# Weight-sum transfers queued behind the attention, and a first chunk that takes the high halves first

## The chip, the cores and the metric

The kernel runs on one core of one Trainium2 chip. The metric is the device time of one execution in microseconds (us), the median of three runs. The engines are named as in the profile: PE (TensorE, matrix products), PEld (its weight loads), DVE (VectorE), ACT (ScalarE), POOL (GpSimd), and SP (SyncE), which here only issues transfers.

## The reference

One residual decoder block on 512 tokens of width 1024, all in float32: a SwiGLU layer, a mixer, and a second SwiGLU layer, each between two RMS norms.

```python
f = swiglu(rms_norm(h, ffn1_pre_g), ffn1_w_gu, ffn1_w_down)     # D_FF = 2816
h = h + 0.5 * rms_norm(f, ffn1_post_g)
m = hybrid_mixer(rms_norm(h, mix_pre_g), ...)
h = h + rms_norm(m, mix_post_g)
f = swiglu(rms_norm(h, ffn2_pre_g), ffn2_w_gu, ffn2_w_down)
h = h + 0.5 * rms_norm(f, ffn2_post_g)

def hybrid_mixer(u, ...):
    gate, x, q, k, v, g_lru, g_attn = split(u @ w_in)            # 1024 1024 1024 256 256 1024 1024
    y_lru = rg_lru(causal_depthwise_conv(x)) * gelu(gate)
    y_attn = sliding_window_attention_with_sinks(rope(q), rope(k), v)   # window 128, 16 heads, 4 key heads
    merged = sigmoid(g_lru) * (y_lru @ w_proj_lru) + sigmoid(g_attn) * (y_attn @ w_proj_attn)
    return merged @ w_out
```

## The kernel before, in words

**Numbers in two halves.** Every operand of a product is split into a high half (rounded to the matrix engine's float32 form) and a low half (the rest). A product of a weight `w` and activations `u` is three matmuls into one PSUM bank: high by high (line 167), high weight by low activation (168), low weight by high activation (169). This is `mm3`.

**Weights.** They are streamed from HBM in pieces of 128 x 1024 in one fixed order, `worder`. `wload` issues the transfer of a piece into `wraw` from SP's queue (line 105), `wround` casts it to the high half on ACT (line 115), `wsplit` subtracts for the low half on DVE (line 123). `wget` and `wnow` hand out the next pair and keep a few pieces ahead. The number in `w85` or `wraw85` is the place in that order.

**Stages.** First feed-forward layer; a token-wise boundary (norms, then transposition of the normalised tokens into features, `to_features`: eight transposes on PE at line 227, a cast on ACT at 231 for `u2h`, a subtraction on DVE at 232 for `u2l`); the mixer's products with `u2`; the output projection `woX`; a second boundary that makes `u3h` and `u3l`; the second feed-forward layer. The boundaries `b1` and `b2` go through four blocks of 128 tokens, so the features of early tokens are ready while later ones are still in work. For this the first chunks of the next layer (a chunk is 128 output columns, eight pieces of the contraction) are done over the tokens' halves of 256: `first_four` for the mixer's `x` products, `first_six` for the second feed-forward layer's `f2f`. Both call `feat_chunk`, which goes through the eight pieces with the three matmuls of `mm3` at each.

**The mixer's order.** `x`, `k`, `v`, `q0` and `q1`, then eight `gate` chunks, then `q2` and `q3`, then eight `gl` chunks (gate and projection of the recurrent branch: `glg`, `glp`), then eight `ga` chunks (of the attention: `gag`, `gap`), then the output projection. `q_pair` sends its rotated result to DRAM and back in another layout, from SP's queue: a store `q_halves` (line 966) and, when that has landed, four loads into `qt` (line 971). A generator `attend(g, n)` does one attention block, of head group `g` and token block `n`: scores on PE (`at30b` is group 3, block 0; line 988), exponentials on ACT, the normalisation of the scores on POOL (line 1003, `at30s`), transposes and the product with `v`, whose upper half ACT copies (`at03c`) and DVE adds to `ya`; `split_y` then splits `ya` for the `ga` stage. The blocks of groups 0 and 1 are started in the `gate` stage and with `q2`, those of groups 2 and 3 in the `gl` stage; the last is `at33`.

**Sums of weights.** The output projection and the feed-forward layers' second products are done by a scheme with seven products in place of eight, which needs sums of weight blocks. For the output projection there are four, `osum[0]` to `osum[3]`, in DRAM, 1 MB each. They are made by transfers alone:

```python
oplan = ((0, 2, 0), (2, 3, 2), (1, 3, None), (3, 1, None))
```

For `(o, a, b)`, block `a` of `w_o` is copied to `osum[o]`, and then block `b` of it, or `osum[o // 2]` where `b` is None, is added by an accumulating transfer. So `osum[1]` needs `osum[0]` complete, and `osum[3]` needs `osum[1]`. The copies are issued from SP's queue in the `gl` chunks 2 to 5 (line 1107, behind the weight load that was issued last), the accumulations from POOL's queue in the `ga` chunks 0, 2 and 4 (line 1147). They are read again as weights: `osum[1]` first, for the second of the output projection's products.

**What sets the order.** Each engine goes through its own queue in order. The program's scheduler sets the order of the queues from the program text, its dependencies and estimates of its own. `tc.issue_after(i)` keeps what stands under it behind instruction `i`. In the parts that the change touches, POOL has little besides the score normalisations and, at the boundaries, some powers (`rstd`, line 212).

Of the kernel before, what the change touches and what calls it, by code (L numbers as in the profile page):

```python
# [11 lines left out]
ALU = mybir.AluOpType  # L12
# [4 lines left out]
P = 128  # L17
# [24 lines left out]
def hybrid_block_kernel(ctx, tc, x, xt, g1, w_first, gains, gu1, gs1, dn1, w_x, w_gate, w_q, w_k, w_v, w_gl, w_ga, w_pl, w_pa,  # L42
# [191 lines left out]
                keep.append((raw[half][:, :, ts_], bv))  # L234
        return [lambda z=z, bv=bv: A.copy(z, bv) for z, bv in keep]

    def feat_chunk(b, w, u, tok):
        wh, wl = w
        for k in range(KD):
            ks = slice(k * P, (k + 1) * P)  # L240
            mm3(b[:, tok], wh[:, ks], wl[:, ks], at(u, 0, k, tok), at(u, 1, k, tok), k == 0, k == KD - 1)
# [4 lines left out]
    def first_four(u, name, done):  # L246
        first = []
        for i in range(4):
            first.append((wget(), bank(f"{name}{i}")))
        for tok in HALVES:  # L250
            for i, (w, b) in enumerate(first):
                feat_chunk(b, w, u, tok)
                tick()
                if tok is HALVES[1]:
                    done(i, b)

    def first_six(u, name, done, early):
        first = []
        for i in range(6):
            first.append((wnow(), bank(f"{name}{i}")))  # L260
            if i < 5:
                wsplit(wpos[0] + 1)
            feat_chunk(first[i][1], first[i][0], u, HALVES[0])
            tick()
        for i, (w, b) in enumerate(first):
            if i == 2:
                early()
            if i >= 4:
                wsplit(wpos[0] + i - 3)
            feat_chunk(b, w, u, HALVES[1])  # L270
            tick()
            done(i, b)

# [621 lines left out]
    def x_group(gi):  # L895
        a4, m4, bx4 = (b8(f"{n}{gi}", [P, 4, T]) for n in ("la", "lm", "lb"))
        hl.append(m4)
        cr = range(4 * gi, 4 * gi + 4)
        if gi == 0:
            first_four(u2, "x", lambda c, b: start(lru_chunk(c, b, a4, m4, bx4, c == cr[-1])))  # L900
        else:
            for c in cr:
                w = wget()
                b = bank(f"x{c}")
                feat_chunk(b, w, u2, ALL)
                tick()
                start(lru_chunk(c, b, a4, m4, bx4, c == cr[-1]))
# [66 lines left out]
    def attend(g, n, kp, vt, y):  # L974
        nm = f"at{g}{n}"
        nk = 1 if n == 0 else 2
        W = nk * P
        keys = slice((n - nk + 1) * P, (n + 1) * P)
        s = t4(f"{nm}s")[:, :4 * W].rearrange("p (h w) -> p h w", h=4)
        sk = sink[:, 4 * g:4 * g + 4]  # L980
        mx = sm(f"{nm}m", 4)
        for half in range(2):
            b = bank(f"{nm}b{half}")
            for i in range(2):
                q = qts[g][:, 2 * half + i, n * P:(n + 1) * P]
                o = b[:, i * W:(i + 1) * W]
                for sgn in range(2):
                    PE.matmul(o, lhsT=q, rhs=kp[g // 2][:, g % 2, sgn, keys], start=sgn == 0, stop=sgn == 1)
            for i in range(2):
                j = 2 * half + i  # L990
                V.tensor_tensor_reduce(out=s[:, j, :], in0=b[:, i * W:(i + 1) * W], in1=msk[:, 2 * P - W:],
                                       scale=HD ** -0.5, scalar=sk[:, j:j + 1], op0=ALU.add, op1=ALU.max,
                                       accum_out=mx[:, j:j + 1])
        es = sm(f"{nm}e", 4)
        V.tensor_tensor(out=es, in0=sk, in1=mx, op=ALU.subtract)
        V.tensor_scalar_mul(mx, mx, -1.0)
        ss = sm(f"{nm}ss", 4)
        for j in range(4):
            A.activation(s[:, j, :], s[:, j, :], AF.Exp, bias=mx[:, j:j + 1], accum_out=ss[:, j:j + 1])
        A.activation(es, es, AF.Exp)  # L1000
        V.tensor_tensor(out=ss, in0=ss, in1=es, op=ALU.add)
        V.reciprocal(ss, ss)
        G.tensor_tensor(out=s, in0=s, in1=ss.rearrange("p (h o) -> p h o", o=1).broadcast_to([P, 4, W]), op=ALU.mult)
        yield ATT_LAG[0]
        pt = []
        for kb in range(nk):
            b = bank(f"{nm}t{kb}")
            for j in range(4):
                PE.transpose(out=b[:, j * P:(j + 1) * P], in_=s[:, j, kb * P:(kb + 1) * P], identity=ident)
            ph, pl = t2(f"{nm}ph{kb}", F32R), t2(f"{nm}pl{kb}", F32R)  # L1010
            A.copy(ph, b)
            V.tensor_tensor(out=pl, in0=b, in1=ph.bitcast(F32), op=ALU.subtract)
            pt.append((ph, pl))
        yield ATT_LAG[1]
        o = bank(f"{nm}o")
        for kb in range(nk):
            v = vt[:, n - nk + 1 + kb, g].rearrange("p s e -> p (s e)")
            for i in range(2):
                PE.matmul(o, lhsT=v, rhs=pt[kb][i], start=kb + i == 0, stop=kb + i == nk)
        r = g % 2  # L1020
        own, oth = slice(HD * r, HD * r + HD), slice(HD * (1 - r), HD * (1 - r) + HD)
        tmp = t2(f"{nm}c")
        A.copy(tmp[own, :], o[oth, :])
        V.tensor_tensor(out=y[own, :, n * P:(n + 1) * P], in0=o[own, :].rearrange("p (h q) -> p h q", h=4),
                        in1=tmp[own, :].rearrange("p (h q) -> p h q", h=4), op=ALU.add)
# [34 lines left out]
        return s, b  # L1060

    qts = {}
    x_group(0)
    kp = [b8(f"kp{i}", [P, 2, 2, T], F32R) for i in range(2)]
    vt = b8("vt", [P, NT, NKV, 2, HD], F32R)
# [32 lines left out]
    for c in range(KD):  # L1098
        s, b = sig_gate(c, yl, "gl")
        if c % 4 == 0:  # L1100
            m1.append(b8(f"m1{c}", [P, 4, T]))
        V.scalar_tensor_tensor(out=m1[-1][:, c % 4, :], in0=s, scalar=1.0, in1=b, op0=ALU.add, op1=ALU.mult)
        if c == 2:
            start(split_y(y0, "ya0"))
        if 2 <= c < 6:
            with tc.issue_after(wdma[wpos[0]].ins):
                SP.dma_start(osum[oplan[c - 2][0]], w_o[oplan[c - 2][1]])
        next_attend()
        if c % 2 == 1:
            next_attend()  # L1110
# [30 lines left out]
    for c in range(KD):  # L1141
        s, b = sig_gate(c, ya, "ga")
        V.scalar_tensor_tensor(out=s, in0=s, scalar=1.0, in1=b, op0=ALU.add, op1=ALU.mult)  # L1143
        V.tensor_tensor(out=mg[c // 4][:, c % 4, :], in0=s, in1=m1[c // 4][:, c % 4, :], op=ALU.add)
        if c % 2 == 0 and c < 6:
            for o, _, b in (oplan[:2], oplan[2:3], oplan[3:])[c // 2]:
                G.dma_start(osum[o], osum[o // 2] if b is None else w_o[b], accum_op=ALU.add)
        if c == 4:
            oop_split(1, a11)
        if c == 5:  # L1150
            oop_split(7, osum_tile("os3", a11, a21, ALU.subtract))
            oop_split(2, a12, ks=slice(0, 2))
# [213 lines left out]
```

## Time and profile before

| | |
|---|---|
| median of three runs | 1121.56 us (1121.44, 1121.56, 1122.51) |
| the profiled execution | 1122.35 us |
| its span in the trace | 1120.6 us, 16935 instructions |
| mean granted clock of PE | 0.996 |
| busy share of the span | PE 98%, PEld 88%, DVE 80%, ACT 54%, POOL 7% |
| moved between HBM and the core | 238 GB/s over the span |

The time of the profiled execution is 1.75 us longer than the span, which goes from its first instruction to its last. The granted clock is the share of full speed that PE was given. In rows on single instructions the first two numbers are the start and the duration in us, then come engine, line, operation, output and inputs, and in brackets the wait ahead of it with what ended it. In a row of the timeline one group may stand for several instructions (x8). In rows of transfers the last numbers are KB and us from issue to landing. `SPq` and `POOLq` are the queues of transfers that SP and POOL issue.

### The profile page before, as it was taken

What the parts mean: (1) busy time and instruction counts of PE and PEld (TensorE: products, weight loads), DVE (VectorE), ACT (ScalarE), POOL (GpSimd) and SP (SyncE); (2) the same over time, 40 slices, a digit from 0 to 9 for tenths busy, and PEclk for the clock granted to TensorE, in tenths of its full rate; (3) what the DMA queues carried; (4) which work ended last, traced back from release to release, by engine and by line L of the source; (5) the groups of instructions that cost most, each with busy time, mean ns of one, the idle gap of its engine ahead of it and who ended that gap; (6) DMA issues with size and microseconds to landing.
All of it is one profiled execution on the core that took longest, in us unless ns stands there. A gap on an engine that the chain in (4) does not pass through costs nothing. (4 is left out here: it accounts for less than half of the span.)

```text
span 1120.6 us, 16935 instructions
## 1 busy us (share of the span) xinstructions
PE 1102.9 (98%) x6582; PEld 982.5 (88%) x6582; DVE 899.9 (80%) x1357; ACT 602.3 (54%) x1003; POOL 83.0 (7%) x86
## 2 busy tenths in 40 slices
PE   9999999999999999999899999999999999999997
PEld 7889999988878888788688888888999999998885
DVE  6998898889998788988656561579789889888896
ACT  7445555465664757675545441257444455456562
POOL 1000010000000101122122000001000000000000
PEclk9999999999999999999989999999999999999999
DMA  9239999664677173612983440446339999555483
GB/s 362 81 121 263 303 288 301 186 225 132 224 274 263 39 207 115 167 57 101 304 230 108 151 156 22 122 146 240 132 99 284 314 272 307 136 161 189 149 275 118
DMA packets 55295, 213.60 MB, mean 191 GB/s; under 512 B 6576, under 2 KB 6704, under 8 KB 49456
## 3 DMA queue, kind: packets, MB, share of 16 engines
q1 hardware_dynamic: 46864, 171.11, 45.0%
q0 software_dynamic: 4032, 27.26, 12.3%
q10 hardware_dynamic: 4320, 14.16, 3.5%
q8 instruction: 51, 0.84, 0.3%
q14 instruction: 28, 0.23, 0.1%
HBM read 200.98 MB, written 66.06 MB: 238 GB/s over the span
## 5 line engine op out<-in xcount | busy, mean ns | idle before, releaser
L123 DVE TENSOR_TENSOR w<-wraw,w 128x1024 fp32r<-128x1024 f32 x174 | 204.2, 1194 | 24.7 <-ACT w L115 24.4
L115 ACT CAST w<-wraw 128x1024 fp32r<-128x1024 f32 x174 | 169.0, 1012 | 29.4 <-PE glp L169 7.4
L169 PE MATMUL f1X<-u1m,f1W 128*128 128x256 f32 x256 | 72.5, 283 | 0.1
L168 PE MATMUL f1X<-u1m,f1W 128*128 128x256 f32 x256 | 72.4, 283 | 0.0
L167 PE MATMUL f1X<-u1m,f1W 128*128 128x256 f32 x256 | 72.4, 283 | 0.0
L169 PEld LDWEIGHTS f1X<-u1m,f1W 128*128 128x128 f32 x256 | 49.1, 192 | 0.3 <-DVE f1W L361 0.3
L167 PEld LDWEIGHTS f1X<-u1m,f1W 128*128 128x128 f32 x256 | 49.1, 192 | 0.1
L168 PEld LDWEIGHTS f1X<-u1m,f1W 128*128 128x128 f32 x256 | 49.1, 192 | 0.1
L1143 DVE SCALAR_TENSOR_TENSOR gas<-gas,gap 128x512 f32<-128x512 f32 x8 | 5.5, 688 | 45.2 <-PE gap L169 45.2
L169 PE MATMUL f2X<-u3m,f2W 128*128 128x256 f32 x144 | 40.9, 284 | 0.1
L169 PE MATMUL f2X<-u3h,f2W 128*128 128x256 f32 x144 | 40.8, 283 | 0.0
L167 PE MATMUL f2Q<-u3m,f2W 128*128 128x256 f32 x144 | 40.8, 283 | 0.0
L168 PE MATMUL f2Q<-u3m,f2W 128*128 128x256 f32 x144 | 40.8, 283 | 0.0
L169 PE MATMUL f2Q<-u3m,f2W 128*128 128x256 f32 x144 | 40.8, 283 | 0.0
L168 PE MATMUL f2X<-u3l,f2W 128*128 128x256 f32 x144 | 40.8, 283 | 0.0
L167 PE MATMUL f2X<-u3m,f2W 128*128 128x256 f32 x144 | 40.8, 283 | 0.0
L168 PE MATMUL f2X<-u3m,f2W 128*128 128x256 f32 x144 | 40.7, 283 | 0.0
L167 PE MATMUL f2X<-u3h,f2W 128*128 128x256 f32 x144 | 40.7, 283 | 0.0
L167 PE MATMUL f1Q<-u1m,f1W 128*128 128x256 f32 x128 | 36.2, 283 | 0.0
L168 PE MATMUL f1Q<-u1m,f1W 128*128 128x256 f32 x128 | 36.2, 283 | 0.0
L169 PE MATMUL f1Q<-u1m,f1W 128*128 128x256 f32 x128 | 36.2, 283 | 0.0
L168 PE MATMUL f1X<-w,f1y 128*128 128x512 f32 x88 | 34.5, 392 | 0.4 <-DVE w L123 0.4
(867 smaller groups left out, 3802.4 us busy)
## 6 DMA issues: line engine op xcount, KB each, us to landing
wraw<-wsum SPq DMA_DIRECT2D x40, 512.0 KB, 4.3
wsum<-in_dn_dram SPq DMA_DIRECT2D x16, 1024.0 KB, 10.5
wraw<-in_dn_dram SPq DMA_DIRECT2D x30, 512.0 KB, 4.8
f2L<-in_gs_dram SPq DMA_DIRECT2D x18, 512.0 KB, 5.3
f2R<-in_gs_dram SPq DMA_DIRECT2D x18, 512.0 KB, 5.2
wraw<-in_gu_dram SPq DMA_DIRECT2D x16, 512.0 KB, 7.3
f1L<-in_gs_dram SPq DMA_DIRECT2D x16, 512.0 KB, 5.8
f1R<-in_gs_dram SPq DMA_DIRECT2D x16, 512.0 KB, 5.8
```

The costliest lines, as they stand in the source:

```text
L115: A.copy(w[:, 0, :], raws[n])
L123: V.tensor_tensor(out=w[:, 1, :], in0=raws[n], in1=w[:, 0, :].bitcast(F32), op=ALU.subtract)
L167: PE.matmul(o, lhsT=ah, rhs=bh, start=start, stop=False, skip_group_check=reopen)
L168: PE.matmul(o, lhsT=ah, rhs=bl, start=False, stop=False, skip_group_check=reopen)
L169: PE.matmul(o, lhsT=al, rhs=bh, start=False, stop=stop, skip_group_check=reopen)
L1143: V.scalar_tensor_tensor(out=s, in0=s, scalar=1.0, in1=b, op0=ALU.add, op1=ALU.mult)
```

## The change

It has two parts.

**The copies.** SP no longer issues the four copies of `w_o` blocks. POOL does, in the `ga` chunks 0 to 3, under `issue_after` of `norms[-1]`, which is the last score normalisation, `at33s`. The accumulations stay on POOL, one each in the `ga` chunks 1, 2, 3 and 5.

**The first chunk.** `feat_chunk` has a new form, `low_last`: over the eight pieces of the contraction it does high by high and low weight by high activation (lines 244 and 245 of the changed kernel), and then, over the eight again, high weight by low activation (line 247). The number of matmuls is the same. `first_four` and `first_six` use it for their chunk 0, in both halves of the tokens. `first_four` is called for `x0`, `first_six` for `f2f0`.

```diff
--- before.py
+++ after.py
@@ -234,8 +234,18 @@
                 keep.append((raw[half][:, :, ts_], bv))
         return [lambda z=z, bv=bv: A.copy(z, bv) for z, bv in keep]
 
-    def feat_chunk(b, w, u, tok):
+    def feat_chunk(b, w, u, tok, low_last=False):
         wh, wl = w
+        if low_last:
+            for n in range(2 * KD):
+                k = n % KD
+                ks = slice(k * P, (k + 1) * P)
+                if n < KD:
+                    PE.matmul(b[:, tok], lhsT=wh[:, ks], rhs=at(u, 0, k, tok), start=k == 0, stop=False)
+                    PE.matmul(b[:, tok], lhsT=wl[:, ks], rhs=at(u, 0, k, tok), start=False, stop=False)
+                else:
+                    PE.matmul(b[:, tok], lhsT=wh[:, ks], rhs=at(u, 1, k, tok), start=False, stop=k == KD - 1)
+            return
         for k in range(KD):
             ks = slice(k * P, (k + 1) * P)
             mm3(b[:, tok], wh[:, ks], wl[:, ks], at(u, 0, k, tok), at(u, 1, k, tok), k == 0, k == KD - 1)
@@ -249,7 +259,7 @@
             first.append((wget(), bank(f"{name}{i}")))
         for tok in HALVES:
             for i, (w, b) in enumerate(first):
-                feat_chunk(b, w, u, tok)
+                feat_chunk(b, w, u, tok, i == 0)
                 tick()
                 if tok is HALVES[1]:
                     done(i, b)
@@ -260,14 +270,14 @@
             first.append((wnow(), bank(f"{name}{i}")))
             if i < 5:
                 wsplit(wpos[0] + 1)
-            feat_chunk(first[i][1], first[i][0], u, HALVES[0])
+            feat_chunk(first[i][1], first[i][0], u, HALVES[0], i == 0)
             tick()
         for i, (w, b) in enumerate(first):
             if i == 2:
                 early()
             if i >= 4:
                 wsplit(wpos[0] + i - 3)
-            feat_chunk(b, w, u, HALVES[1])
+            feat_chunk(b, w, u, HALVES[1], i == 0)
             tick()
             done(i, b)
 
@@ -1000,7 +1010,8 @@
         A.activation(es, es, AF.Exp)
         V.tensor_tensor(out=ss, in0=ss, in1=es, op=ALU.add)
         V.reciprocal(ss, ss)
-        G.tensor_tensor(out=s, in0=s, in1=ss.rearrange("p (h o) -> p h o", o=1).broadcast_to([P, 4, W]), op=ALU.mult)
+        norms.append(G.tensor_tensor(out=s, in0=s, in1=ss.rearrange("p (h o) -> p h o", o=1).broadcast_to([P, 4, W]),
+                                     op=ALU.mult))
         yield ATT_LAG[0]
         pt = []
         for kb in range(nk):
@@ -1060,6 +1071,7 @@
         return s, b
 
     qts = {}
+    norms = []
     x_group(0)
     kp = [b8(f"kp{i}", [P, 2, 2, T], F32R) for i in range(2)]
     vt = b8("vt", [P, NT, NKV, 2, HD], F32R)
@@ -1102,9 +1114,6 @@
         V.scalar_tensor_tensor(out=m1[-1][:, c % 4, :], in0=s, scalar=1.0, in1=b, op0=ALU.add, op1=ALU.mult)
         if c == 2:
             start(split_y(y0, "ya0"))
-        if 2 <= c < 6:
-            with tc.issue_after(wdma[wpos[0]].ins):
-                SP.dma_start(osum[oplan[c - 2][0]], w_o[oplan[c - 2][1]])
         next_attend()
         if c % 2 == 1:
             next_attend()
@@ -1142,9 +1151,13 @@
         s, b = sig_gate(c, ya, "ga")
         V.scalar_tensor_tensor(out=s, in0=s, scalar=1.0, in1=b, op0=ALU.add, op1=ALU.mult)
         V.tensor_tensor(out=mg[c // 4][:, c % 4, :], in0=s, in1=m1[c // 4][:, c % 4, :], op=ALU.add)
-        if c % 2 == 0 and c < 6:
-            for o, _, b in (oplan[:2], oplan[2:3], oplan[3:])[c // 2]:
-                G.dma_start(osum[o], osum[o // 2] if b is None else w_o[b], accum_op=ALU.add)
+        if c < 4:
+            o, a, _ = oplan[c]
+            with tc.issue_after(norms[-1].ins):
+                G.dma_start(osum[o], w_o[a])
+        if c in (1, 2, 3, 5):
+            o, _, b = oplan[min(c, 4) - 1]
+            G.dma_start(osum[o], osum[o // 2] if b is None else w_o[b], accum_op=ALU.add)
         if c == 4:
             oop_split(1, a11)
         if c == 5:
```

All lines behind the new ones have moved down: 966 is 976, 971 is 981, 1003 is 1013, 1147 is 1157 (copies) and 1160 (accumulations).

SP's queue where the `gl` stage begins, before. `q_halves` and `qt` are the stores and loads of the rotated queries, L105 the weight loads, L1107 the copies:

```order
L966 DMA q_halves2_5379<-q2st_5318 128x2048
L105 DMA wraw83_5461<-in_w_pl_dram 128x1024
L105 DMA wraw84_5521<-in_w_gl_dram 128x1024
L1107 DMA osums_75<-in_w_o_dram 128x2048
L971 DMA qt2_5437<-q_halves2_5379 32x4x512 x4
L966 DMA q_halves3_5516<-q3st_5452 128x2048
L105 DMA wraw85_5594<-in_w_pl_dram 128x1024
L105 DMA wraw86_5634<-in_w_gl_dram 128x1024
L1107 DMA osums_75<-in_w_o_dram 128x2048
L971 DMA qt3_5556<-q_halves3_5516 32x4x512 x4
L105 DMA wraw87_5721<-in_w_pl_dram 128x1024
```

The same place after:

```order
L976 DMA q_halves2_5379<-q2st_5318 128x2048
L105 DMA wraw83_5461<-in_w_pl_dram 128x1024
L105 DMA wraw84_5521<-in_w_gl_dram 128x1024
L981 DMA qt2_5437<-q_halves2_5379 32x4x512 x4
L976 DMA q_halves3_5516<-q3st_5452 128x2048
L981 DMA qt3_5556<-q_halves3_5516 32x4x512 x4
L105 DMA wraw85_5594<-in_w_pl_dram 128x1024
L105 DMA wraw86_5634<-in_w_gl_dram 128x1024
L105 DMA wraw87_5721<-in_w_pl_dram 128x1024
```

The four copies are gone (two more stood a few rows further on), and the loads of `qt3` now stand ahead of `wraw85` and `wraw86`. On ACT, where the scheduler moves with it, the casts of `w82` to `w84` now stand ahead of the copy `at03c`, not behind it.

POOL's queue in the `gl` stage, before. L1003 are the score normalisations, L1147 the accumulations:

```order
L942 TENSOR_TENSOR q3m0_5442<-q3m0_5442,q3m3_5445 128x512
L1147 DMA osums_75<-in_w_o_dram 128x2048
L1003 TENSOR_TENSOR at20s_5563<-at20s_5563,at20ss_5582 128x512
L1147 DMA osums_75<-in_w_o_dram 128x2048
L1003 TENSOR_TENSOR at30s_5662<-at30s_5662,at30ss_5681 128x512
L1003 TENSOR_TENSOR at21s_5690<-at21s_5690,at21ss_5709 128x1024
L1147 DMA osums_75<-osums_75 128x2048
L1003 TENSOR_TENSOR at31s_5795<-at31s_5795,at31ss_5814 128x1024
L1147 DMA osums_75<-osums_75 128x2048
L1003 TENSOR_TENSOR at22s_5924<-at22s_5924,at22ss_5943 128x1024
L1003 TENSOR_TENSOR at32s_5952<-at32s_5952,at32ss_5971 128x1024
L1003 TENSOR_TENSOR at23s_6079<-at23s_6079,at23ss_6098 128x1024
```

POOL's queue from the end of the `gl` stage to the boundary `b2`, after:

```order
L1013 TENSOR_TENSOR at32s_5950<-at32s_5950,at32ss_5969 128x1024
L1013 TENSOR_TENSOR at23s_6076<-at23s_6076,at23ss_6095 128x1024
L1013 TENSOR_TENSOR at33s_6211<-at33s_6211,at33ss_6230 128x1024
L1157 DMA osums_75<-in_w_o_dram 128x2048 x4
L1160 DMA osums_75<-in_w_o_dram 128x2048 x2
L1160 DMA osums_75<-osums_75 128x2048 x2
L212 TENSOR_TENSOR b2p0r_7234<-b2p0e_7232,mhalf_142 128x1
L212 TENSOR_TENSOR b2p1r_7241<-b2p1e_7239,mhalf_142 128x1
```

All eight transfers now stand between `at33s` and the first power of the boundary, four copies (L1157), two accumulations of `w_o` and two of another sum (L1160).

PE's queue at the first chunk of the second feed-forward layer, second half of the tokens, before. `b2ntp3` are the transposes of the last block of tokens, `u3h0` and `u3l0` the high and low halves of the first four pieces of the features:

```order
L227 MATMUL b2ntp30_7592<-ident_135,b2un3_7397 128x128 x4
L227 MATMUL b2ntp31_7599<-ident_135,b2un3_7397 128x128 x4
L167 MATMUL f2f0_7423<-u3h0_7226,w124_7222 128x256
L168 MATMUL f2f0_7423<-u3l0_7228,w124_7222 128x256
L169 MATMUL f2f0_7423<-u3h0_7226,w124_7222 128x256
```

The same place after (`u3l1` has the low halves of the other four pieces):

```order
L227 MATMUL b2ntp30_7592<-ident_135,b2un3_7397 128x128 x4
L227 MATMUL b2ntp31_7599<-ident_135,b2un3_7397 128x128 x4
L244 MATMUL f2f0_7423<-u3h0_7226,w124_7222 128x256
L245 MATMUL f2f0_7423<-u3h0_7226,w124_7222 128x256
...
L247 MATMUL f2f0_7423<-u3l0_7228,w124_7222 128x256 x4
L247 MATMUL f2f0_7423<-u3l1_7229,w124_7222 128x256 x4
```

Between the two parts shown the pair of L244 and L245 goes on to the eighth piece. The low halves are now read from the seventeenth matmul on, not from the second; the transposes stand where they stood.

PE's queue at the mixer's first chunk, before. `b1ntp2` are the transposes of the third block of tokens:

```order
L169 MATMUL f1X1_2687<-w49_3402,f1y42_3391 128x512
L167 MATMUL x0_3667<-u2h0_2736,w50_3500 128x256
L227 MATMUL b1ntp20_3710<-ident_135,b1un2_3529 128x128 x4
L227 MATMUL b1ntp21_3717<-ident_135,b1un2_3529 128x128 x4
L167 MATMUL x1_3673<-u2h0_2736,w51_3511 128x256
L167 MATMUL x2_3679<-u2h0_2736,w52_3662 128x256
L168 MATMUL x0_3667<-u2l0_2738,w50_3500 128x256
L169 MATMUL x0_3667<-u2h0_2736,w50_3500 128x256
```

The same place after:

```order
L244 MATMUL x0_3667<-u2h0_2736,w50_3500 128x256
L245 MATMUL x0_3667<-u2h0_2736,w50_3500 128x256
L227 MATMUL b1ntp20_3710<-ident_135,b1un2_3529 128x128 x4
L227 MATMUL b1ntp21_3717<-ident_135,b1un2_3529 128x128 x4
L244 MATMUL x0_3667<-u2h1_2737,w50_3500 128x256
L245 MATMUL x0_3667<-u2h1_2737,w50_3500 128x256
```

Ahead of these stand six more of `x0`'s matmuls with `u2h0`. The transposes stand behind eight matmuls of `x0` with high halves in place of one, and eight more follow ahead of the other chunks.

## The prediction

> **What bounds the kernel now.** I read the page's first part, then TensorE's waits, then the timeline around the longest wait, then the DMA rows there.
>
> ```profile
> PE 1102.9 (98%) x6582; PEld 982.5 (88%) x6582; DVE 899.9 (80%) x1357; ACT 602.3 (54%) x1003; POOL 83.0 (7%) x86
> ```
>
> TensorE (PE) is busy for all but 17.7 us of the 1120.6 us span. A change that adds and removes no arithmetic can win only there, or where the clock is low.
>
> ```profile
> PE at30b L988 <- DMA qt<-q_halves: 4.7, 1, 4.7
> ...
> PE f2f L168 <- DVE u3l L232: 0.7, 2, 0.3
> PE f2f L167 <- ACT u3h L231: 0.7, 2, 0.4
> PE f2f L169 <- DVE w L123: 0.5, 2, 0.3
> ```
>
> The columns are total, times, longest. One wait stands out: the scores of the first attention block that reads `qt3` wait 4.7 us for its load. The next rows are short waits of the second feed-forward layer's first chunks for the features' high halves (`u3h`), low halves (`u3l`) and the weights.
>
> ```profile
> 555.88 0.39 PE L169 MATMUL glp<-ylh,w 128*128 128x512 f32 x1
> 560.92 1.94 PE L988 MATMUL at30b<-kp,qt 128*128 128x128 f32 x8 [4.65 <-DMA qt<-q_halves]
> 564.47 0.63 PE L167 MATMUL glg<-u2h,w 128*128 128x512 f32 x1
> ...
> 566.58 0.39 PE L169 MATMUL glg<-u2h,w 128*128 128x512 f32 x1
> ```
>
> ```profile
> 556.00:561.00 5.00, 0.35 (x3) 0.11 (x1) 0.69 (x1) 2.18 (x4) 0.84 (x1) 0.87 1.06 236
> 561.00:567.00 6.00, 6.00 (x23) 5.50 (x24) 3.71 (x22) 2.88 (x13) 0.84 (x1) 0.54 1.06 294
> ```
>
> The last three columns of the stretches are granted clock, DMA share and GB/s. The wait costs twice. A mean clock of 0.87 over 5 us is half clock for 1.3 us, so the clock fell at about 559.7, some 3.4 us after PE stopped; 0.54 over 6 us is half clock for 5.5 us more. The DMA engines are full throughout.
>
> ```profile
> 590.50 1.12 PE L988 MATMUL at22b<-kp,qt 128*128 128x256 f32 x8
> 591.45 1.12 PE L988 MATMUL at32b<-kp,qt 128*128 128x256 f32 x8
> ```
>
> At full clock eight such score matmuls take 0.95 us from start to start. From 560.92 to 566.58 stand two groups of eight and five 512-wide matmuls (0.23 us each at full clock): 2 x 0.95 + 5 x 0.23 = 3.05 us, against 5.66 measured. So the half clock costs 2.6 us.
>
> **Part 1: the copies.** The four 1 MB copies of `w_o` leave SP's queue, and all eight transfers of the weight sums go behind `at33s` in POOL's queue.
>
> ```profile
> 527.96 0.33 SPq L966 DMA_DIRECT2D q_halves<-q2st  x1
> ...
> 532.40 2.11 SPq L971 DMA_DIRECT2D qt<-q_halves  x4
> 538.65 0.34 SPq L966 DMA_DIRECT2D q_halves<-q3st  x1
> ...
> 546.85 1.76 SPq L971 DMA_DIRECT2D qt<-q_halves  x4
> ```
>
> ```profile
> osums<-in_w_o_dram POOLq DMA_DIRECT2D x1, 1024.0 KB, 12.2
> osums<-in_w_o_dram SPq DMA_DIRECT2D x1, 1024.0 KB, 15.4
> qt<-q_halves SPq DMA_DIRECT2D x4, 256.0 KB, 11.3
> ```
>
> q3's store goes out at 538.65 and its four loads can be issued only when it has landed, at 546.85. In that stretch an accumulation and a copy of the sums run on the same DMA engines (12.2 and 15.4 us to landing), and the loads take 11.3 us in the median. From store to use it is 560.92 - 538.65 = 22.3 us.
>
> ```profile
> 456.73 0.34 SPq L966 DMA_DIRECT2D q_halves<-q1st  x1
> 470.32 1.08 PE L988 MATMUL at10b<-kp,qt 128*128 128x128 f32 x8 [1.30 <-DMA qt<-q_halves]
> ```
>
> q1 made the same trip with no sums beside it, and PE waited for its last load: 470.32 - 456.73 = 13.6 us. q2 had one copy of the sums beside it:
>
> ```profile
> DMA to landing us min/median/max: 7.7/8.8/9.1
> ```
>
> Its loads, four from 532.40 on, issued over 2.11 us and landing within 9.1, were there by 543.6 at the latest, at most 15.7 us after the store. After the change no sum runs beside q3, and its loads stand ahead of `wraw85` and `wraw86`, not behind them. I take 13.6 us, the nearest row, so `qt3` is there at 552.2; with q2's 15.7 at 554.3; with no help at all at 560.9. PE reaches `at30b` at 555.88 + 0.23 = 556.1. Both nearer rows are in time, with 3.9 and 1.8 us to spare, so the wait goes whole: 4.7 us, and with it the half clock: 2.6 us. Bounds: 0 and 7.3; I take 7.3.
>
> The late work next is `wraw85` and `wraw86`, now issued after `qt3`'s loads. `w85` is used by `glp3`, some twenty microseconds of PE work after `at30b`; that work hides it, at 0. The three casts that now stand ahead of `at03c` on ScalarE delay only `ya`, which no PE wait in the list touches: 0. POOL's four accumulations no longer stand between the score normalisations, which waited for VectorE or ScalarE anyhow: 0.
>
> ```profile
> 628.90 1.90 POOL L1003 TENSOR_TENSOR at33s<-at33s,at33ss 128x1024 f32<-128x1024 f32 x1 [14.79 <-ACT gls L1051]
> osums<-in_w_o_dram SPq DMA_DIRECT2D x1, 1024.0 KB, 18.1
> 746.21 0.39 PE L167 MATMUL woX<-w,oy 128*128 128x512 f32 x1
> ```
>
> Where they go: POOL is free behind `at33s` (ends 630.8, so 623.5 after the change) until the boundary far behind `woX`. The sum that is read first (`osum[1]`, for the product at 746.21) needs a copy, an accumulation into `osum[0]` and one of its own. Even at the slowest landing here, 18.1 us each, that is 54 us, to about 682 with POOL's issues; it must be there some 15 us (load, cast, split) ahead of 738.9. About 40 us are spare: 0. If that cover were gone, each microsecond would be one of PE's.
>
> **Part 2: high halves first.** Same matmuls, same weight loads. It can win where the first chunk waits for low halves.
>
> ```profile
> 797.79 0.38 PE L167 MATMUL f2f<-u3h,w 128*128 128x256 f32 x1 [0.24 <-ACT u3h L231]
> 798.51 0.39 PE L168 MATMUL f2f<-u3l,w 128*128 128x256 f32 x1 [0.34 <-DVE u3l L232]
> 798.74 0.28 PE L169 MATMUL f2f<-u3h,w 128*128 128x256 f32 x1
> 797.77 1.29 DVE L232 TENSOR_TENSOR u3l<-b2ntp,u3h 128x512 fp32r<-128x512 f32 x2 [2.46 <-ACT u3h L231]
> 786.62 0.39 PE L169 MATMUL f2f<-u3h,w 128*128 128x256 f32 x1 [0.28 <-DVE w L123]
> ```
>
> Second token half of `f2f`: the third matmul starts 0.95 us after the first. With high halves only, the second starts after 0.23 and the third 0.12 later, at 0.35; the lows, ready at 799.06, are wanted at 799.8. The gain is 0.6 us, and PE is without a wait behind it for long, so it stays. The first token half has the same pattern, but PE then waits at 786.62 for a weight split that stands in VectorE's queue behind the normalisation of later tokens; what PE gains it waits there. I take 0, with 0.6 as the other end.
>
> ```profile
> 342.19 0.39 PE L167 MATMUL x<-u2h,w 128*128 128x256 f32 x1 [0.24 <-ACT u2h L231]
> ...
> 344.87 0.39 PE L168 MATMUL x<-u2l,w 128*128 128x256 f32 x1 [0.15 <-DVE u2l L232]
> ...
> 353.74 1.29 PE L227 MATMUL b1ntp<-ident,b1un 128*128 128x128 f32 x8 [0.34 <-DVE b1un L546]
> ```
>
> Mixer: before, 4 of `x`'s matmuls and the third token block's transposes are issued by 345.09. After, 16 fit (twelve more at 0.12), so PE is 1.4 us ahead. But the last block's transposes at 353.74 wait for VectorE's `b1un`, whose queue is unchanged and waits for nothing of this stage's matmuls. PE idles there 1.4 us longer: 0, with 1.4 as the other end. The idle, about 2 us, lies between 1.30 us at `at10b`, which cost no clock (1.08 us for its eight), and 4.65, which cost 2.6; being nearer the first, 0, and 2.6 lost stays the bound.
>
> Sum: 4.7 + 2.6 + 0.6 = 7.9 us. The profiled execution took 1122.35 us (span 1120.6), so it would take 1114.4; the median of the runs is 0.8 lower, 1121.56, and gives **1113.7 us**.
>
> [...]
>
> **The rivals.**
> Residual wait (0.10): `qt3` comes later than 556.1, since the store and 1 MB of weights still share the engines. For it: the store's 8.2 us to the loads' issue at 538.65, against 4.4 for q2. Against: the two trips above. At half the delay saved (22.3 to 18 us, arrival 556.7 or a little after) PE waits a microsecond or two, without half clock: 1115 to 1116.
>
> The copies were not the cause (0.05): the loads are slow from the weights alone, or the wait stays 4.7 us. Only 0.6 remains: 1121.0. Against: the 11.3 us median is twice what the DMA engines needed when q1's PE wait was 1.3.
>
> More than forecast (0.06): VectorE's queue moves up with PE at both boundaries, 1.4 + 0.6 more: 1111.7. Against: those waits are released by VectorE alone.
>
> Slower (0.05): the sums come late to `woX`. The chain is serial on one queue and shares the engines with the gates' weights. It decides from the point where the copy and two accumulations need more than about 92 us from 623.5; to undo the 7.9 and 2.3 more it must need over 100, three times 34 us, twice the slowest row. The time would be 1124 or more. [...]
>
> **How the numbers follow.** The forecast has 0.74, the others as given. No change is told from noise within 0.2%, 2.2 us, here. Faster: 0.74 + 0.10 + 0.06 = 0.90, less 0.02 for a residual wait that keeps nearly all: 0.88. Same: 0.05 + 0.02 = 0.07. Slower 0.05. Range: down to 1111.7 with both gains of part 2, up to 1116.8, the residual case with part of the half clock or the 2.6 us bound at 353.74.
>
> **What would show it.** Right: no wait of `at30b` for `qt`, one clock of 1.00 from 550 to 570, the loads of `qt3` landing in some 6 to 8 us, POOL's eight issues behind `at33s`, `f2f`'s wait for `u3l` gone in both halves, and a longer wait of the last `b1ntp` near 353.7. Wrong: a wait for `qt` that is left, a new PE wait for `w` in the `ga` chunks or at `woX`, or matmuls of lines 244 and 245 that stand more than 0.12 us apart.

## The result, and the profile after

The changed kernel took 1115.59 us in the median of four runs (1113.61 to 1116.43), the kernel before 1121.50 us (four runs, 1120.91 to 1122.51). The ratio is 0.9944, with a 95% interval of 0.9927 to 0.9961: faster by 0.56%, or 5.9 us. The forecast was 1113.7 us, within 1111.7 to 1116.8. The profiled execution of the changed kernel took 1116.43 us, the one before 1122.35 us: again 5.9 us.

The first lines of the page after, which answer to those of before:

```profile
span 1114.6 us, 16931 instructions
PE 1100.9 (99%) x6582; PEld 981.9 (88%) x6582; DVE 901.2 (81%) x1357; ACT 602.5 (54%) x1003; POOL 85.0 (8%) x90
```

PE is now busy for all but 13.7 us of the span, where it was 17.7. TensorE's waits after (total, times, longest, in us):

```profile
PE b1ntp L227 <- DVE b1un L556: 1.8, 1, 1.8
...
PE f2f L169 <- DVE w L123: 0.9, 2, 0.6
PE at10b L998 <- DMA qt<-q_halves: 0.8, 1, 0.8
PE f2f L244 <- ACT u3h L231: 0.7, 2, 0.4
...
PE f2g L169 <- DVE w L123: 0.3, 1, 0.3
```

The wait of `at30b`, 4.7 us, is gone, and so is the wait of `f2f` for `u3l`. In their place stand three: 1.8 us of the first boundary's transposes for `b1un` (0.3 before), 0.9 us of `f2f` for a weight split (0.5 before), and 0.3 us of `f2g` for another (none before).

**Where the copies' part shows.** SP's queue and PE after, around `q3`, and the issues of that stretch with KB and us to landing:

```profile
540.12 0.34 SPq L976 DMA_DIRECT2D q_halves<-q3st  x1
545.44 1.73 SPq L981 DMA_DIRECT2D qt<-q_halves  x4
```

```profile
557.22 0.39 PE L169 MATMUL glp<-ylh,w 128*128 128x512 f32 x1
557.45 1.00 PE L998 MATMUL at30b<-kp,qt 128*128 128x128 f32 x8
558.29 1.17 PE L998 MATMUL at21b<-kp,qt 128*128 128x256 f32 x8
559.30 0.40 PE L167 MATMUL glg<-u2h,w 128*128 128x512 f32 x1
```

```profile
q_halves<-q3st SPq DMA_DIRECT2D x1, 1024.0 KB, 5.3
qt<-q_halves SPq DMA_DIRECT2D x4, 256.0 KB, 5.2
```

The store lands 5.3 us after its issue in place of 8.1, the loads in 5.2 in the median in place of 11.3. The fourth load of `qt3` lands at 553.0, 12.9 us after the store was issued, where it had been 22.1 (560.78 against 538.65, the last load's issue at 548.17 and its 12.6 us); `at30b` follows the matmul ahead of it without a gap. From `at30b` to the first `glg` it is 1.85 us, at full clock, against 3.55 before.

**Where the high halves' part shows.** PE at the first boundary after, and the stretches behind it, with the granted clock in the third column from the end:

```profile
352.12 0.28 PE L169 MATMUL x<-u2h,w 128*128 128x256 f32 x1
354.19 1.29 PE L227 MATMUL b1ntp<-ident,b1un 128*128 128x128 f32 x8 [1.78 <-DVE b1un L556]
```

```profile
354.00:356.00 2.00, 1.78 (x14) 1.60 (x15) 1.23 (x3) 1.08 (x3) 0.00 (x0) 0.95 0.69 266
356.00:358.00 2.00, 2.00 (x11) 2.00 (x11) 1.75 (x3) 2.00 (x4) 0.00 (x0) 0.50 0.56 172
358.00:360.00 2.00, 2.00 (x14) 2.00 (x14) 2.00 (x3) 0.93 (x1) 0.00 (x0) 0.69 0.61 154
```

PE has done its work 1.4 us earlier and stands idle for it, as forecast. What was not forecast is what follows: half clock for 3.4 us. Here the changed kernel lost 1.5 us. In the trace of before the same stretches are at 1.00, for example:

```profile
356.00:358.00 2.00, 2.00 (x19) 2.00 (x19) 1.74 (x3) 2.00 (x3) 0.00 (x0) 1.00 0.91 250
```

The second feed-forward layer after:

```profile
780.46 0.38 PE L169 MATMUL f2f<-u3h,w 128*128 128x256 f32 x1 [0.65 <-DVE w L123]
...
791.62 0.39 PE L244 MATMUL f2f<-u3h,w 128*128 128x256 f32 x1 [0.24 <-ACT u3h L231]
791.84 0.28 PE L245 MATMUL f2f<-u3h,w 128*128 128x256 f32 x1
...
809.91 0.50 PE L169 MATMUL f2g<-u3h,w 128*128 128x512 f32 x1 [0.29 <-DVE w L123]
```

In the second half of the tokens the matmuls follow each other without the gap at 798.51, and PE is 0.6 us ahead. 18 us later it waits at `f2g` for the split of a weight whose place in VectorE's queue has not moved.

The same work in both profiled executions, start in us:

| work | before | after | after less before |
|---|---|---|---|
| `b1ntp3`, transposes of the last block | 353.74 | 354.19 | +0.4 |
| first gate of the recurrence (`r`) | 368.55 | 370.47 | +1.9 |
| `at10b` | 470.32 | 471.76 | +1.4 |
| `at30b` | 560.92 | 557.45 | -3.5 |
| `at20t` | 570.93 | 564.77 | -6.2 |
| `f2g` | 815.77 | 808.99 | -6.8 |
| `f2X`, the layer's next products | 826.69 | 820.49 | -6.2 |
| end of the span | 1120.6 | 1114.6 | -6.0 |

The +0.4 is not of the change. In the trace's record of the granted clock full speed begins at 7.65 us of the span here and at 6.75 before. Ahead of that the first four `f1f` matmuls here stand 0.43 us apart (5.89 to 7.60), behind it the next eight 0.23 us (8.57 to 10.41), so 0.9 us more are some 0.4 us, and `f1X` starts at 73.02 here and at 72.58 before. Then the half clock costs 1.5. At `at10b` 0.5 come back, but not from the change either: there PE waits for `q1`'s trip through DRAM, and that trip took 13.0 us here and 13.5 before. In the fourteen profiled executions of this document it took 12.4 to 13.5 us, 13.0 and 13.4 in the two traces of the changed kernel. With the copies alone, where no half clock stands ahead of it, the wait is as short:

```profile
PE at10b L998 <- DMA qt<-q_halves: 0.7, 1, 0.7
```

The wait at `at30b` brings 4.9 and its half clock 2.7; `f2f` brings 0.6 and `f2g` takes it back. So the mixer's part costs 1.5 us and nothing returns, where two expectations below still have 1.0 net.

### The profile page after: what moved, and what is told of

Its sections match the earlier page's. It is cut to its first block, busy times and chain, and to the rows that moved or that the text cites. A ratio compares the mean times of both kernels' runs of the same rounds, so it can differ in the third digit from the quotient of the medians.

```text
span 1114.6 us, 16931 instructions
## 1 busy us (share of the span) xinstructions
PE 1100.9 (99%) x6582; PEld 981.9 (88%) x6582; DVE 901.2 (81%) x1357; ACT 602.5 (54%) x1003; POOL 85.0 (8%) x90
## 3 DMA queue, kind: packets, MB, share of 16 engines
q0 software_dynamic: 4608, 31.46, 13.4%
## 5 line engine op out<-in xcount | busy, mean ns | idle before, releaser
L123 DVE TENSOR_TENSOR w<-wraw,w 128x1024 fp32r<-128x1024 f32 x174 | 204.3, 1193 | 24.6 <-ACT w L115 24.2
L168 PE MATMUL f2X<-w,f2y 128*128 128x512 f32 x88 | 34.5, 392 | 0.4 <-DVE w L123 0.4
```

The costliest lines, as they stand in the source:

```text
L123: V.tensor_tensor(out=w[:, 1, :], in0=raws[n], in1=w[:, 0, :].bitcast(F32), op=ALU.subtract)
L168: PE.matmul(o, lhsT=ah, rhs=bl, start=False, stop=False, skip_group_check=reopen)
```

## The experiments

**The parts apart.** Four kernels beside each other on one chip; there the kernel before took 1121.56 us. The runs further on were taken on two other chips, where it took 1121.96 and 1121.47 us; each ratio is against the kernel before on the same chip.

The copies alone:

```diff
-                feat_chunk(b, w, u, tok, i == 0)          # first_four; first_six likewise
+                feat_chunk(b, w, u, tok)
```

> Only the copies move; every first chunk goes through its eight pieces with three matmuls each, as before. Theory (the copies took away the whole wait at at30b with its half clock, 4.9 + 2.7 us by the two traces, and the high halves first cost the mixer boundary 1 us net): 1121.5 - 7.6 = 1113.9, a b1ntp wait of 0.3 us as before, no half clock near 355 us, mean clock 0.999. Rival 1 (the high halves first are innocent; what the changed kernel lacks against the forecast lies in the copies or in the loads of the first microseconds): 1115.6, as the changed kernel. Rival 2 (the high halves first bring 0.6 us in the second feed-forward layer that stay): 0.6 slower than a kernel with them in that layer alone.

Measured: 1114.44 us (1113.77 to 1114.89, five runs), ratio 0.9933 (0.9920 to 0.9947). The clock is at 1.00 from 350 to 360 us, with a mean of 0.999 in the profiled execution. The theory holds: the copies alone are faster than the whole change.

The high halves alone (copies and accumulations as before):

```diff
-            with tc.issue_after(norms[-1].ins):
-                G.dma_start(osum[o], w_o[a])
+            with tc.issue_after(wdma[wpos[0]].ins):       # back in the gl loop
+                SP.dma_start(osum[oplan[c - 2][0]], w_o[oplan[c - 2][1]])
```

> Only the first chunks take the high halves first; copies and accumulations stay where they were before. Theory: the wait at at30b stays at 4.7 us with 6.8 us of half clock, PE waits 1.8 us at b1ntp in place of 0.3 and runs at half clock for 3.4 us behind it, of which 0.5 us come back at at10b's wait; the 0.6 us of f2f's second half are given back at f2g: 1121.5 + 1.0 = 1122.5. Rival 1 (innocent in the mixer, and the 0.6 us stay): 1120.9. Rival 2: no change, 1121.5.

Measured: 1123.07 us (1120.61 to 1125.30, eleven runs), ratio 1.0012 (1.0003 to 1.0021): slower by 0.12%. Its waits show both stalls at once:

```profile
PE at30b L998 <- DMA qt<-q_halves: 4.8, 1, 4.8
PE b1ntp L227 <- DVE b1un L556: 1.8, 1, 1.8
```

The copies, and the high halves in the second feed-forward layer alone:

```diff
-                feat_chunk(b, w, u, tok, i == 0)          # first_four only
+                feat_chunk(b, w, u, tok)
```

> The copies moved, and the high halves first in the second feed-forward layer alone; the mixer's first chunk as before. Theory: as with the copies alone, 1113.9, clock 0.999: f2f's wait for u3l is gone in the second half of the tokens, but f2g waits 0.3 us and more for a weight split whose place in VectorE's queue has not moved, and f2X starts no earlier. Rival 1 (the mixer is innocent): 1115.6, as the changed kernel. Rival 2 (the 0.6 us stay): 1113.3.

Measured: 1114.31 us (1113.31 to 1114.92), ratio 0.9932 (0.9919 to 0.9944): as the copies alone. In the trace `f2g` starts at 806.83 and `f2X` at 818.35, 0.6 us more between them than before; the 0.6 us are given back there.

The changed kernel again:

> The changed kernel once more, on the same chip as the three parts. Theory: 1115.6, with mean clock 0.998 where the clock falls behind the b1ntp wait and 0.999 with a time nearer 1114 where an execution is spared that; 1.0 to 1.7 us slower than with the high halves first in the second feed-forward layer alone. Rival 1: the same as that kernel within 0.3 us.

Measured: 1116.20 us, ratio 0.9945 (0.9932 to 0.9957). Four of five executions lie between 1116.07 and 1116.36 us with a mean clock of 0.998; one took 1113.56 us at 0.999. So the mixer's part costs 1.9 us by the medians (1116.20 against 1114.31); the traces have 1.5, as the table further on shows. A mean of 0.999 leaves no room for 3.4 us at half clock, so that execution was spared it, as the theory has it. It does not show the cause: no trace was taken of it, and it is 2.6 us faster than the others, more than the 1.5.

**Is it the idle time that takes the clock down?** 14 matmuls by zeros were to fill it:

```diff
+                if i == 3 and tok is HALVES[0]:
+                    for _ in range(FILL):                 # FILL = 14
+                        PE.matmul(b[:, tok], lhsT=w[0][:, :P], rhs=zero, start=False, stop=True, ...)
```

> The changed kernel with 14 matmuls more by a tile of zeros (256 columns, 0.12 us each) behind the first half of the mixer's first four chunks, where PE waited 1.8 us at b1ntp. They add nothing to the sums and move no other work ahead of the transposes; some matmuls of the stage behind come in another order. Theory (the idle time itself takes the clock down): the wait shrinks to 0.1 to 0.3 us, there is no half clock near 355 us, mean clock 0.999 in all executions, and the time goes to that of the copies alone, 1114.4. Rival 1 (something else there takes the clock down): half clock for 3.4 us as before, 1116.2. Rival 2 (the fillers delay the transposes): 1116 or more without half clock.

Measured: 1117.56 us, ratio 0.9960 (0.9945 to 0.9974). This did not test it: the transposes stand ahead of the fourth chunk, so the fillers stood behind the wait.

```profile
353.67 1.34 PE L230 MATMUL b1ntp<-ident,b1un 128*128 128x128 f32 x8 [1.79 <-DVE b1un L562]
359.17 1.82 PE L268 MATMUL x<-zero,w 128*128 128x256 f32 x14
```

It shows that PE's work there counts in full: 14 x 0.12 = 1.7 us, and in the trace all that comes behind the `x` products stands 1.7 us later than in the changed kernel (table below). Behind the third chunk (`i == 2`) they stand ahead:

> The 14 matmuls by a tile of zeros again, now behind the third of the mixer's first four chunks, so that they stand ahead of the last block's transposes in PE's queue; nothing else in any queue moves against the changed kernel. Theory (the idle time takes the clock down): b1ntp waits 0.1 to 0.3 us, no half clock near 355 us, the transposes start when they did, and the time is 1116.2 - 1.7 = 1114.5, in all executions. Rival (something else there takes the clock down, or matmuls by zeros don't hold it up): half clock for 3.4 us stays, 1116.2.

```profile
351.46 1.82 PE L268 MATMUL x<-zero,w 128*128 128x256 f32 x14
353.40 1.29 PE L230 MATMUL b1ntp<-ident,b1un 128*128 128x128 f32 x8
```

```profile
356.00:358.00 2.00, 2.00 (x19) 2.00 (x18) 1.74 (x3) 2.00 (x3) 0.00 (x0) 1.00 0.72 234
```

Measured: 1114.44 us, ratio 0.9937 (0.9923 to 0.9950). The changed kernel, on another chip, had 1116.20 and 0.9945 (0.9932 to 0.9957): the times alone hardly tell the two apart. The traces do. The table has the starts of the first matmul of `f1X`, ahead of the boundary, and of `kk`, the `k` product behind the `x` products, in us:

| kernel | `f1X` | `kk` | between |
|---|---|---|---|
| before | 72.58 | 371.10 | 298.5 |
| the copies alone | 72.62 | 371.15 | 298.5 |
| the changed kernel | 73.02 | 373.02 | 300.0 |
| the changed kernel again | 72.54 | 372.56 | 300.0 |
| fillers behind the wait | 72.52 | 374.18 | 301.7 |
| fillers ahead of it | 72.25 | 370.76 | 298.5 |

Matmuls that compute nothing make this stretch 1.5 us shorter than without them, since they hold the clock (1.00 from 356 to 358 us, 0.50 in the changed kernel), and it is then as short as with the copies alone. The theory is shown.

**What freed the loads?** The copies in POOL's queue, but early, behind `at13s`:

```diff
-            with tc.issue_after(norms[-1].ins):
+            with tc.issue_after(norms[7].ins):
```

> As the copies alone, but POOL issues the four copies behind at13s (near 528 us), so that the sums run beside the stores and loads of q2 and q3 again, from POOL's queue. SP's queue has no copy, and qt3's loads stand where the program's scheduler puts them. Theory (it is the later time that frees the loads, not the other queue): PE waits for qt at at20b or at30b again, 5 us or more with the half clock behind it, 1118 to 1128, likeliest 1122. Rival (SP's queue was the cause: the loads stood behind its copies): no wait at either, 1114.4.

```profile
564.62 1.94 PE L998 MATMUL at20b<-kp,qt 128*128 128x128 f32 x8 [21.40 <-DMA qt<-q_halves]
```

```profile
qt<-q_halves SPq DMA_DIRECT2D x4, 256.0 KB, 21.4
q_halves<-q3st SPq DMA_DIRECT2D x1, 1024.0 KB, 24.6
wraw<-in_w_pl_dram SPq DMA_DIRECT2D x1, 512.0 KB, 25.4
```

Measured: 1138.42 us, ratio 1.0142 (1.0126 to 1.0159). The sign is as the theory says, the size beyond its range (1118 to 1128): with four copies at once, and behind them the accumulations, which POOL's queue brings forward with them (from 535.0 us on), `qt2`'s loads take 21.4 us in the median, `q3`'s store 24.6, and a weight piece 25.4. SP's queue is free of copies here, so it is the transfers beside, not the queue they stand in.

The copies in SP's queue as before, only the accumulations late:

```diff
+            with tc.issue_after(wdma[wpos[0]].ins):       # gl loop, as before
+                SP.dma_start(osum[oplan[c - 2][0]], w_o[oplan[c - 2][1]])
...
+                with tc.issue_after(norms[-1].ins):       # ga loop
                     G.dma_start(osum[o], ..., accum_op=ALU.add)
```

> As the copies alone, but the copies stay in SP's queue in the gl stage as before; only the accumulations go behind at33s. Theory (the sums' share of the transfer engines beside q3 counts, copy and accumulation alike): q3 has one copy beside it, as q2 had before, where store to last load took 15.2 us against 22.1 for q3; so qt3 is there at 538.7 + 15.2 = 553.9, ahead of 556, no wait at at30b: 1114.4, at most 1115.5. Rival 1 (the copies in SP's queue alone make the wait): 4.7 us and its half clock stay, 1121.5. Rival 2 (half of each): a wait of 1 to 2.5 us, 1116 to 1118.

```profile
538.47 0.34 SPq L976 DMA_DIRECT2D q_halves<-q3st  x1
545.61 1.73 SPq L981 DMA_DIRECT2D qt<-q_halves  x4
547.38 0.43 SPq L105 DMA_DIRECT2D wraw<-in_w_pl_dram  x1
547.92 0.36 SPq L105 DMA_DIRECT2D wraw<-in_w_gl_dram  x1
548.33 0.50 SPq L1119 DMA_DIRECT2D osums<-in_w_o_dram  x1
```

Measured: 1114.58 us, ratio 0.9930 (0.9916 to 0.9945), as the theory says, but not for its reason: the scheduler put the second copy behind `qt3`'s loads too. The first copy had landed by 538.8, so `q3`'s store had no sum beside it, and the second went out at 548.3, 1.4 us behind the last load's issue. The trip took 14.7 us. What a copy alone, or an accumulation alone, beside `q3` would cost stays open. That copies stay in SP's queue does no harm by itself, in this order.

The weights ahead of `qt3`'s loads again, `wraw85` and `wraw86` between store and loads:

```diff
-        SP.dma_start(dr, st)
+        sent = SP.dma_start(dr, st)
         yield 1
+        if m == 3:
+            with tc.issue_after(sent.ins):
+                wload(87)
...
-            SP.dma_start(qt[32 * r:32 * r + 32].bitcast(F32), src[r])
+            with tc.issue_after(wdma[86 if m == 3 else 0].ins):
+                SP.dma_start(qt[32 * r:32 * r + 32].bitcast(F32), src[r])
```

> As the copies alone, but wraw85 and wraw86 (1 MB of weights) are issued between q3's store and q3's loads again, as before the change; nothing else moves. Theory (the sums beside q3 were the cause, the weights count little): qt3 is there by 554.5, store to last load at most 16 us, no wait at at30b: 1114.4. Rival (the place of qt3's loads ahead of these weights is part of the gain): store to last load 17 to 19 us, a wait of 0.5 to 3 us at at30b: 1115 to 1118.

```profile
537.18 0.34 SPq L976 DMA_DIRECT2D q_halves<-q3st  x1
537.61 0.38 SPq L105 DMA_DIRECT2D wraw<-in_w_pl_dram  x1
538.04 0.91 SPq L105 DMA_DIRECT2D wraw<-in_w_gl_dram  x1
542.89 1.75 SPq L985 DMA_DIRECT2D qt<-q_halves  x4
```

Measured: 1114.13 us, ratio 0.9935 (0.9921 to 0.9948). The last load lands at 550.8, 13.7 us after the store's issue, and `at30b` does not wait. With 1 MB of weights beside it the trip is 0.8 us longer than in the changed kernel's trace, but in the nine profiled executions whose order there is that of the changed kernel it took 12.1 to 13.9 us, so no share of the weights can be seen. Before the change, with the same weights and the sums beside it, it took 22.1: the 8.4 us between go to the sums.

**Where does the cover of the sums end?** The sums made twice:

```diff
+        if c == 5:
+            for o, a, b in oplan:
+                G.dma_start(osum[o], w_o[a])
+                G.dma_start(osum[o], osum[o // 2] if b is None else w_o[b], accum_op=ALU.add)
```

> As the copies alone, but POOL makes the four sums twice, one set behind the other, with the same result. One set took 46.8 us (624.57 to 671.41) in the changed kernel, and the first sum was read at 701.64. Theory (the cover behind the sums ends where the first sum comes later than about 715): the second set goes one transfer after the other at about 10 us, osum[1] is ready near 720, its load waits some 18 us at the head of SP's queue, and PE waits at the second product of the output projection: 1114.4 + 5 = 1119, between 1115 and 1126. Rival 1 (the cover is longer than the second set): 1114.4. Rival 2 (the second set takes the transfer engines from the ga weights as well): waits of PE for w in the ga chunks, over 1126.

```profile
693.33 0.82 POOL L1164 DMA_DIRECT2D osums<-osums  x1 [19.50 <-DMA osums<-in_w_o_dram]
...
701.86 0.80 SPq L105 DMA_DIRECT2D wraw<-osums  x2
```

Measured: 1113.83 us, ratio 0.9930 (0.9915 to 0.9945): no loss, rival 1. I had laid the second set end to end at 10 us each; it overlapped the first, `osum[1]` was ready at 701.8 and not at 720, and its load went out then, 2.6 us later than with the copies alone (both counted from the first `f1X` matmul). No wait for `w` is in its list beyond those of the copies alone. The end of the cover was not found.

**Can the high halves pay?** With the changed kernel as the start, the last block's transposes one chunk later, so that `x3`'s first half fills the wait:

```diff
-FEATURE_LAG = {"b1": (7, 9, 7, 3), "b2": (1, 1, 5, 6)}
+FEATURE_LAG = {"b1": (7, 9, 7, 4), "b2": (1, 1, 5, 6)}
```

> The changed kernel with the last block's transposes of the first boundary one chunk later in PE's queue: x3's first half, 24 matmuls of 0.12 us, now stands ahead of them and not behind. Theory: PE works through the stretch where it waited 1.8 us; the transposes start at about 355.0 in place of 354.2; x0's second half, which then needs their casts, starts at about 356.5 in place of 358.1 at full clock (359.7 as it was); no half clock: 1116.2 - 3.0 = 1113.2. Rival 1 (VectorE takes the gain back later, as in the second feed-forward layer): 1114.4, as the copies alone. Rival 2 (PE now waits as long for the casts behind the transposes): 1115 to 1116.

```profile
356.30 0.39 PE L244 MATMUL x<-u2h,w 128*128 128x256 f32 x1 [0.24 <-ACT u2h L231]
370.75 0.50 PE L167 MATMUL r<-xch,bd 128*128 128x512 f32 x1 [1.28 <-ACT xch L870]
```

Measured: 1113.81 us (1113.15 to 1114.74), ratio 0.9930 (0.9917 to 0.9944). The idle time and the half clock are gone (the matmuls stand 0.12 us apart from 356.5 on) and `x0`'s second half starts at 356.3, as expected. But 14 us later PE waits 1.3 us for ScalarE's `xch`: rival 1, with ScalarE in VectorE's place: from `f1X` to `kk` it is 298.4 us, against 298.5 with the copies alone. What is won is the clock, not the order.

The same, with the splits of `f2g`'s first weights earlier in VectorE's queue, the first of them by two instructions:

```diff
-            if i >= 4:
-                wsplit(wpos[0] + i - 3)
+            if i >= 3:
+                wsplit(wpos[0] + min(i - 2, 2))
```

> As the run before, and the split of the first weight piece of f2g stands two instructions (1.4 us) earlier in VectorE's queue. Theory: f2g's wait of 0.3 us for that split is gone and f2X starts 0.6 us earlier against f2f, so the 0.6 us of the high halves in the second half of f2f stay: 1112.6, 0.6 below the run before, which the times alone can hardly tell and the starts in the trace can. Rival: VectorE's queue takes it back further on, no change against the run before.

```profile
807.06 0.39 PE L169 MATMUL f2g<-u3h,w 128*128 128x512 f32 x1
...
817.50 0.28 PE L167 MATMUL f2X<-u3h,f2W 128*128 128x256 f32 x1
```

Measured: 1113.23 us (1112.77 to 1113.65), ratio 0.9925 (0.9913 to 0.9938), the lowest median of all. `f2g` has no wait, and `f2X` starts 10.9 us behind `f2g`'s first matmul (806.59) as before the change, and not 11.5. From `f2f`'s second half (789.22) to the end of the span it is 322.4 us, against 323.0 in the run before: the 0.6 us stay. The times alone leave it open against the run before; the starts tell it.

## Why the prediction was right, and where it was off

**The sign, and the copies' term: right.** The wait at `at30b` went whole and its half clock with it, 4.9 + 2.7 us against 4.7 + 2.6. The trip from store to last load took 12.9 us where I took 13.6, and was 4.4 us early. From POOL's queue the same copies, with the accumulations behind them, cost 21.4 us at `at20b` when issued early, and nothing when issued late. (In the 2.6 us of the half clock the prediction took 0.95 us for each group of eight score matmuls from rows of 256 columns, where `at30b` has 128; the changed kernel's rows give 0.84 and 1.01 us for the two groups, which moves the term by 0.05.)

**The rivals of the copies' part: none came.** No residual wait; that the copies were not the cause is excluded by the kernels with each part alone.

**The cover of the sums: right.** `osum[1]` was there 35 us after the first copy's issue (659.5), estimated at 54 at most, all four after 46.8 us. With the sums doubled `osum[1]` was ready 42 us later, about the 40 us that the prediction called spare, and it cost nothing. In the rival of the late sums the 92 us and the 34 us are not worked out; by the prediction's own rows the cover is 746.21 - 7.3 - 15 - 623.5 = 100 us, and the copy and two accumulations took 35.

**The 0.6 us of `f2f`'s second half: wrong.** The step that failed is "PE is without a wait behind it for long, so it stays". I looked for waits in the trace of before, where PE was the later one; what counts is how much earlier the other side was. The split for `f2g` was less than 0.6 us ahead of PE, and its place moves with VectorE's queue, not with PE. I had applied just this to the first half of the tokens, where the gain went into the wait at 786.62 (0.28 before, 0.65 after), and not to the second.

**The mixer, 0: wrong, with the cause named.** PE's extra idle time was forecast, but the step "being nearer the first, 0, and 2.6 lost stays the bound" failed. 1.78 us of idle time cost a half clock of 3.4 us, which is 1.5 us of time, where the prediction took 0; the matmuls by zeros show it. Laying an idle time between two others and taking the cost of the nearer one was the weak step: nothing showed that the cost goes that way. The sum with the two terms of part 2 as measured is 4.9 + 2.7 + 0 - 1.5 = 6.1 us against 5.9; the forecast had 7.9. The stated range held the time, since its upper end allowed for a loss of up to 2.6 us at just this wait. The rival that forecast more, with both gains of part 2, was wrong: VectorE releases those waits alone, as I held against it.

## What to carry to other kernels

Put large transfers that nobody waits for where no short chain of store and load is on the path; the queue that issues them mattered less here than the stretch in which they move (the loads of the queries took 11.3 us beside a copy from SP's queue and an accumulation from POOL's, 21.4 with all of the sums in POOL's queue, and 5.2 with none beside them). Work that PE did earlier ahead of a wait that another engine ends won nothing here, and at `b1ntp` the 1.78 us that PE then stood idle also cost 3.4 us at half clock: before such an edit, ask how far ahead that other engine is at the next two or three meetings, and what PE has at hand to fill the gap. Where two kernels are one or two microseconds apart, read the distance between two starts in each trace, not only the medians.

## What the runs showed of the hardware

Idle times of PE and the granted clock behind them, from the traces of the kernel before and of the changed kernel:

| where | PE idle, us of the span | length, us | granted clock |
|---|---|---|---|
| `at10b`, before | 469.02 to 470.32 | 1.30 | 1.00 to 480 |
| `b1ntp`, after | 352.41 to 354.19 | 1.78 | 1.00, then 0.50 from 355.8 to 359.2 |
| `at30b`, before | 556.27 to 560.92 | 4.65 | 1.00, then 0.50 from 559.7 to 566.5 |
| behind the last matmul, after | 1108.22 to 1114.6 | 6.4 | 1.00 to 1113.57, then 0.50 |

So the half clock lasted 3.4 us behind the 1.78 us of idle time and 6.8 us behind the 4.65; the 1.30 us at `at10b` had none behind them. At `b1ntp` PE had been at work again for 1.6 us when the clock fell. In the second trace of the changed kernel the half clock there lasted 3.4 us as well (0.72, 0.50 and 0.93 in the three stretches of 2 us from 354 on), and with the fillers behind the wait the matmuls stand 0.21 us apart from 355.0 to 358.0 and 0.12 from 358.2 on.

The length of the idle time does not decide alone. At the end of the changed kernel PE has been idle for 5.35 us, and the clock is still at full speed (the columns are as above, the first group PE):

```profile
1106.75:1110.16 3.41, 1.47 (x7) 0.89 (x5) 1.06 (x3) 0.69 (x2) 0.55 (x1) 1.00 0.00 0
1110.16:1113.57 3.41, 0.00 (x0) 0.00 (x0) 1.17 (x2) 0.00 (x0) 0.00 (x0) 1.00 0.41 154
```

What separates the cases stays open.

The first `f1X` matmul starts at 72.25 to 73.02 us in the table further up, so these profiled executions differ by up to 0.8 us ahead of the boundary `b1`.
